# Hybrid encoder layer on one core: the first norm's operation on GpSimd, products of zeros in a pause, and the gating's norm scale and bias moved behind the mixing

## The chip, the cores and the metric

The kernel runs on 1 core of one Trainium2 chip. The time is the device time of one execution in microseconds (us). The core's engines have queues of their own: TensorE (PE, with its weight loads PEld), VectorE (DVE), ScalarE (ACT), GpSimd (POOL) and SyncE (SP), which here only issues DMAs. An engine works through its queue in order; semaphores tie the queues together.

## The reference, cut to what matters

One layer, one sequence of 512 tokens with 2048 channels, all in float32:

```
mod = silu(c) @ w_ada + b_ada;  shift, scale, gate = split(mod, 3)
h = layernorm(x) * (1 + scale) + shift
u, v, z_a, q, k, v_b, z_b = split(h @ w_in)            # 7168 columns
vg = layernorm(gelu(v), per channel group of 128) * norm_g + norm_b
sv = einsum('gpq,bnqgc->bnpgc', w_s, vg) + b_s          # mixes the 128 tokens of a chunk
y_a = gelu(u) * sv * silu(z_a)
y_b = neighbourhood_attention(q, k, v_b, rpb) * silu(z_b)
out = layernorm(alpha * x + (1 + gate) * (concat(y_a, y_b) @ w_out)) * ln_g + ln_b
```

For a channel c of group g the mixing is linear, so that the sum over q of w_s[p,q] * (n[q,c] * norm_g[c] + norm_b[c]) equals norm_g[c] * (the sum over q of w_s[p,q] * n[q,c]) + norm_b[c] * (the sum over q of w_s[p,q]).

## The kernel before, in words

Every float32 product is made of three products in a rounded float type: an operand is split into a high part (`h_hi`, `whi`) and a low part (`h_lo`, `wlo`), and high by high, high by low and low by high are summed in PSUM (`mm3`, L225; `mm_vz`, L238). ACT makes the high part of a weight block (L195), DVE or POOL the low part (L197).

**Start.** The four token tiles of x (128 tokens each) are loaded. For a tile n, `statistics` (L431, L432, DVE) gives mean and variance, `inverse` (L435, L436, POOL) the inverse deviation, and `normalise` (L444) the normalised tile in four quarters of 512 columns: all four on POOL for tiles 0 and 1, two on POOL and two on DVE for tiles 2 and 3. Each quarter is transposed by four TensorE products with the identity (L448) and copied back by ACT (L449), which gives channels by tokens.

**Modulation.** `w_ada` is read in tiles `wada` (ring of ADA = 6, L324). The 128 channels of k tile 0 get their scale and shift on TensorE (`ada_tensor`, L350, 64 hardware products); those of the other 15 k tiles on DVE (`ada_vector`, L367, L369, L375), closed by a product with ones (`ada_end`, L383) and an add (L384). `make_h` then makes `h_hi` and `h_lo` of the k tile (ACT L396 or L399/L400, DVE L397 and L401). `ada_before` says how many weight blocks of the plan are loaded before each `wada` tile; `pump` issues both kinds on SP in that order.

**First phase.** Projections start as soon as k tiles 0 and 1 exist (`first_segment`): all products that need k tile 0, then `advance(6)`, which closes the modulation of k tile 1, then those that need k tile 1. PSUM: `psm` is the ring of four banks that hold `res` (the open sums of VZ0), `psx` the ring of partial sums.

**Gating.** `sgu` runs twice, for two halves of 4 channel groups: DVE statistics per group (L552, L553), variance plus epsilon (L121, DVE), its inverse root (L122, POOL), the normalisation (L557, DVE), times `gB` and plus `bB` (L559, L560, POOL), then per group the mixing product (L566), plus the bias (L567, DVE), times y (L570, DVE). The first half runs beside the last segment of the first phase, where `psx` sums of z_a are taken up by DVE (L760, L765) and a bank of that ring becomes the fifth bank of `psm`; the second runs beside the last projection.

The queues' order is written by a scheduler from the program's order, except for instructions in `pin(...)`, which keep it. After the first phase come attention, the output projection and the last norm.

## Time and profile before

| | |
|---|---|
| time, median of 3 runs | 949.42 us (949.05 to 949.64) |
| the profiled execution's own time | 947.96 us |
| its span (first to last instruction) | 946.2 us |
| PE busy | 891.0 us (94%) |
| PEld, DVE busy | 773.6 us (82%), 603.9 us (64%) |
| POOL, ACT busy | 354.1 us (37%), 321.6 us (34%) |
| DMA | 145.6 MB, mean 154 GB/s |

Times in the profile are microseconds from the span's start. A product's row starts when it enters the array; its neighbour may start before it has ended, so what products cost is read from the distance of their starts. A bracket at the end of a row says how long the engine was idle before it, and what ended the wait. [...]

### The profile page before, as it was taken

What the parts mean: (1) busy time and instruction counts of PE and PEld (TensorE: products, weight loads), DVE (VectorE), ACT (ScalarE), POOL (GpSimd) and SP (SyncE); (2) the same over time, 40 slices, a digit from 0 to 9 for tenths busy, and PEclk for the clock granted to TensorE, in tenths of its full rate; (3) what the DMA queues carried; (4) which work ended last, traced back from release to release, by engine and by line L of the source; (5) the groups of instructions that cost most, each with busy time, mean ns of one, the idle gap of its engine ahead of it and who ended that gap; (6) DMA issues with size and microseconds to landing.
All of it is one profiled execution on the core that took longest, in us unless ns stands there. A gap on an engine that the chain in (4) does not pass through costs nothing.

```text
span 946.2 us, 11802 instructions
## 1 busy us (share of the span) xinstructions
PE 891.0 (94%) x4468; PEld 773.6 (82%) x4468; DVE 603.9 (64%) x843; ACT 321.6 (34%) x397; POOL 354.1 (37%) x242
## 2 busy tenths in 40 slices
PE   2879999989998999999999999999999999999994
PEld 1768888788796898889888988899888888888883
DVE  3175898773456655575767867786867834252667
ACT  1226323313353143452527152624154421122300
POOL 6634546623558152605242543444246000000035
PEclk9989999999999899999999999999999999999997
DMA  9479988963432223344444555444433383323313
GB/s 303 124 222 306 298 266 264 311 201 112 157 89 76 76 84 96 101 146 127 153 150 132 168 156 147 154 123 144 134 98 104 112 313 131 112 83 103 105 51 127
DMA packets 107787, 145.60 MB, mean 154 GB/s; under 512 B 6993, under 2 KB 78801, under 8 KB 106961
## 3 DMA queue, kind: packets, MB, share of 16 engines
q1 hardware_dynamic: 103120, 134.25, 44.9%
q10 hardware_dynamic: 4610, 10.59, 3.2%
q8 instruction: 35, 0.57, 0.3%
q14 instruction: 22, 0.18, 0.1%
HBM read 140.62 MB, written 4.19 MB: 153 GB/s over the span
## 4 chain that ended last, share of the span: by engine, by line
PE 81%; POOL 7%; DVE 5%; issue 3%; DMA 2%; ACT 1%; POOLq 0%; SPq 0%; ACTq 0%; DVEq 0%
PE psm L225 52%; PE psx L225 14%; PE psm L238 8%; POOL xt L444 2%; PE ada L350 1%; POOL wlo L197 1%; POOL xr L878 1%; DVE ada L369 1%; DMA raw<-in_w_in_dram 1%; PE psx L687 1%; PE psx L639 1%; PE psx L566 1%; PE psx L638 1%; PE psx L685 1%; POOL xr L879 1%
## 5 line engine op out<-in xcount | busy, mean ns | idle before, releaser
L195 ACT CAST whi<-raw 128x1024 fp32r<-128x1024 f32 x133 | 139.0, 1049 | 355.6 <-PE psm L225 225.1
L197 DVE TENSOR_TENSOR wlo<-raw,whi 128x1024 fp32r<-128x1024 f32 x95 | 131.9, 1391 | 160.2 <-ACT whi L195 144.7
L225 PE MATMUL psm<-h_hi,whi 128*128 128x512 f32 x444 | 175.8, 396 | 0.4 <-DVE klo L592 0.4
L225 PE MATMUL psm<-h_lo,whi 128*128 128x512 f32 x444 | 174.4, 393 | 0.0
L225 PE MATMUL psm<-h_hi,wlo 128*128 128x512 f32 x444 | 174.3, 393 | 0.0
L197 POOL TENSOR_TENSOR wlo<-raw,whi 128x1024 fp32r<-128x1024 f32 x38 | 91.6, 2416 | 114.7 <-ACT whi L195 82.2
L225 PE MATMUL psm<-whi,h_hi 128*128 128x512 f32 (+1 forms) x296 | 114.7, 388 | 0.0
L225 PE MATMUL psm<-wlo,h_hi 128*128 128x512 f32 (+1 forms) x296 | 114.0, 385 | 0.0
L225 PE MATMUL psm<-whi,h_lo 128*128 128x512 f32 (+1 forms) x296 | 114.0, 385 | 0.0
L225 PEld LDWEIGHTS psm<-h_hi,wlo 128*128 128x128 f32 x444 | 84.0, 190 | 18.1
L225 PEld LDWEIGHTS psm<-h_hi,whi 128*128 128x128 f32 x444 | 84.3, 190 | 16.0 <-issue 0.6
L225 PEld LDWEIGHTS psm<-h_lo,whi 128*128 128x128 f32 x444 | 84.4, 190 | 15.2
L238 PE MATMUL psm<-whi,h_hi 128*128 128x256 f32 x248 | 72.3, 293 | 8.0 <-DVE s L760 4.9
L238 PE MATMUL psm<-whi,h_lo 128*128 128x256 f32 x248 | 71.9, 292 | 4.6 <-DVE h_lo L401 4.6
L122 POOL TENSOR_TENSOR rs<-vareps,mhalf 128x1 f32<-128x1 f32 x4 | 4.4, 1098 | 184.5 <-DVE vareps L121 184.5
L238 PE MATMUL psm<-wlo,h_hi 128*128 128x256 f32 x248 | 71.9, 290 | 0.2 <-DVE wlo L197 0.2
L369 DVE SCALAR_TENSOR_TENSOR ada<-wada,c_sb,ada 128x512 f32<-128x512 f32 (+1 forms) x104 | 69.1, 715 | 2.1 <-DMA wada<-in_w_ada_dram 1.8
L225 PEld LDWEIGHTS psm<-wlo,h_hi 128*128 128x128 f32 x296 | 63.5, 215 | 8.4
L225 PEld LDWEIGHTS psm<-whi,h_lo 128*128 128x128 f32 x296 | 63.4, 214 | 8.5
L225 PEld LDWEIGHTS psm<-whi,h_hi 128*128 128x128 f32 x296 | 63.4, 214 | 8.5
L225 PE MATMUL psx<-h_hi,whi 128*128 128x512 f32 x160 | 63.5, 397 | 2.3 <-DVE y_b L475 2.0
L225 PE MATMUL psx<-h_hi,wlo 128*128 128x512 f32 x160 | 62.5, 390 | 1.3 <-POOL wlo L197 1.3
(199 smaller groups left out, 1690.9 us busy)
## 6 DMA issues: line engine op xcount, KB each, us to landing
wada<-in_w_ada_dram SPq DMA_DIRECT2D x128, 256.0 KB, 5.2
raw<-in_w_in_dram SPq DMA_DIRECT2D x128, 256.0 KB, 3.2
raw<-in_w_in_dram SPq DMA_DIRECT2D x48, 512.0 KB, 4.3
rawg<-in_w_ada_dram SPq DMA_DIRECT2D x32, 512.0 KB, 4.4
raw<-in_w_out_dram SPq DMA_DIRECT2D x32, 512.0 KB, 3.7
xt<-in_x_dram SPq DMA_DIRECT2D x8, 512.0 KB, 8.5
xr<-in_x_dram ACTq DMA_DIRECT2D x4, 1024.0 KB, 7.4
tt<-in_rpb_dram ACTq DMA_DIRECT2D x16, 128.0 KB, 2.2
```

What stands on the lines that cost most here:

```text
L195: nc.scalar.copy(out=hi, in_=raw)
L197: eng.tensor_tensor(out=low, in0=raw, in1=hi.bitcast(F32), op=ALU.subtract)
L225: nc.tensor.matmul(ps, lhsT=a, rhs=b, start=first and j == 0, stop=last and j == 2)
L238: nc.tensor.matmul(ps[:, t * w:(t + 1) * w], lhsT=a, rhs=b[:, cs], start=first and t == 0 and j == 0, stop=last and t == 1 and j == 2)
L350: pin(nc.tensor.matmul(pc[s], lhsT=wt[:, j - j0, s, :], rhs=c_sb[:, j:j + 1], start=j == 0, stop=j == NK - 1))
L369: nc.vector.scalar_tensor_tensor(out=even if j == NK - 2 else acc, in0=wt[:, j - j0], scalar=cj, in1=acc, op0=ALU.mult, op1=ALU.add)
L444: eng.tensor_scalar(out=xn[:, cs], in0=xn[:, cs], scalar1=mv[:, n, 0:1], scalar2=rstd[:, n:n + 1], op0=ALU.subtract, op1=ALU.mult)
L566: nc.tensor.matmul(ps[:, tok(n)], lhsT=v[n][:, tok(g)], rhs=wsT[:, g, :], start=True, stop=True)
L638: nc.tensor.matmul(po, lhsT=k2[:, h, keys], rhs=q2[:, h, q], start=True, stop=False)
L639: nc.tensor.matmul(po, lhsT=klo[:, h, keys], rhs=q2[:, h, q], start=False, stop=True)
L685: nc.tensor.matmul(ps[:, q], lhsT=v_hi[:, t, h, :], rhs=hi[:, sl], start=t == 0, stop=False, skip_group_check=True)
L687: nc.tensor.matmul(ps[:, q], lhsT=v_hi[:, t, h, :], rhs=lo[:, sl], start=False, stop=t == 3, skip_group_check=True)
```

## The change

1. **First norm.** DVE negates the mean and adds epsilon to the variance after each tile's statistics; POOL's inverse is one instruction in place of two; `normalise` adds the negative mean and multiplies (was: subtract and multiply), and keeps program order.
2. **Zeros.** A region of `h_lo` is set to zero at the start, and 14 products with these zeros as weights are added into `res[0]` ahead of `advance(6)` in `first_segment`. They change no value.
3. **Loads of `w_ada`.** The ring has 7 tiles, and for k tiles from 4 on a `wada` tile is due two weight blocks earlier.
4. **Gating.** The normalised v is mixed without `gB` and `bB` (8 POOL instructions less in each half). One more product per half, a 128x128 block of ones by the half's four spatial weights, gives their column sums; four DVE instructions (128x128) make norm_b times these sums plus b_s; the bias add behind each mixing product becomes multiply (norm_g) and add. norm_g and norm_b are loaded once as columns, 128 x 8 each.

```diff
-ADA = 6
+ADA = 7
+ZEROS = 14
...
-    one = const.tile([P, 1], F32, name="one")
-    nc.vector.memset(one, 1.0)
+    ones = const.tile([P, P], F32R, name="ones")
+    nc.vector.memset(ones.bitcast(F32), 1.0)
+    one = ones.bitcast(F32)[:, 0:1]
+    gb = const.tile([P, 2, 8], F32, name="gb")
+    nc.scalar.dma_start(out=gb[:, 0, :], in_=sgu_g)
+    nc.scalar.dma_start(out=gb[:, 1, :], in_=sgu_b)
...
-            ada_before += [2 if k0 == 1 else 5 * k0 // 2] * (4 * nk)
+            ada_before += [2 if k0 == 1 else 5 * k0 // 2 - 2 * (k0 > 2)] * (4 * nk)
...
+        zeros = h_lo[:, NK - 1, :P]
+        nc.vector.memset(zeros.bitcast(F32), 0.0)
...
             nc.vector.bn_aggr(out=mv[:, n, :], in_=st)
+            nc.vector.tensor_scalar(out=mv[:, n, 0:1], in0=mv[:, n, 0:1], scalar1=-1.0, scalar2=None, op0=ALU.mult)
+            nc.vector.tensor_scalar(out=mv[:, n, 1:2], in0=mv[:, n, 1:2], scalar1=EPS, scalar2=None, op0=ALU.add)
 
         def inverse(n):
-            nc.gpsimd.tensor_scalar(out=rstd[:, n:n + 1], in0=mv[:, n, 1:2], scalar1=1.0, scalar2=EPS, op0=ALU.mult, op1=ALU.add)
-            nc.gpsimd.tensor_tensor(out=rstd[:, n:n + 1], in0=rstd[:, n:n + 1], in1=mhalf[:, 0:1], op=ALU.pow)
+            nc.gpsimd.tensor_tensor(out=rstd[:, n:n + 1], in0=mv[:, n, 1:2], in1=mhalf[:, 0:1], op=ALU.pow)
...
-                eng.tensor_scalar(out=xn[:, cs], in0=xn[:, cs], scalar1=mv[:, n, 0:1], scalar2=rstd[:, n:n + 1],
-                                  op0=ALU.subtract, op1=ALU.mult)
+                pin(eng.tensor_scalar(out=xn[:, cs], in0=xn[:, cs], scalar1=mv[:, n, 0:1], scalar2=rstd[:, n:n + 1],
+                                      op0=ALU.add, op1=ALU.mult))
...
                 mm3(two[i], wv, i, 0, False, True, False)
+
+            for _ in range(ZEROS):
+                nc.tensor.matmul(res[0], lhsT=zeros, rhs=h_hi[:, 0, :], start=False, stop=False)
             advance(6)
...
-            nc.gpsimd.tensor_tensor(out=v[n], in0=v[n], in1=gB, op=ALU.mult)
-            nc.gpsimd.tensor_tensor(out=v[n], in0=v[n], in1=bB, op=ALU.add)
-            yield
+            yield
+        ps = bank()
+        nc.tensor.matmul(ps, lhsT=ones.bitcast(F32), rhs=flat, start=True, stop=True)
+        for g in range(4):
+            nc.vector.scalar_tensor_tensor(out=bs[:, g, :], in0=ps[:, tok(g)], scalar=gb[:, 1, half * 4 + g:half * 4 + g + 1], in1=bs[:, g, :],
+                                           op0=ALU.mult, op1=ALU.add)
         yield
...
-            nc.vector.tensor_tensor(out=sv, in0=ps.rearrange("p (n q) -> p n q", n=4),
-                                    in1=bs[:, g:g + 1, :].to_broadcast([P, 4, P]), op=ALU.add)
+            nc.vector.scalar_tensor_tensor(out=sv, in0=ps.rearrange("p (n q) -> p n q", n=4), scalar=gb[:, 0, half * 4 + g:half * 4 + g + 1],
+                                           in1=bs[:, g:g + 1, :].to_broadcast([P, 4, P]), op0=ALU.mult, op1=ALU.add)
```

What the change moves is seen in the queues' orders. Line numbers are those of the kernel in question (L435, L436, L444 before are L445, L453 after; L225 is L231, L238 is L244, L383 is L391, L122 is L128, L197 is L203). First TensorE in the pause of the first k tiles, before:

```order
L225 MATMUL psx<-whi,h_hi 128x512
L225 MATMUL psx<-wlo,h_hi 128x512
L225 MATMUL psx<-whi,h_lo 128x512
L383 MATMUL ada_111<-one,gate_89 128x1 x2
L238 MATMUL psm<-whi,h_hi 128x256
L238 MATMUL psm<-wlo,h_hi 128x256
```

And after:

```order
L231 MATMUL psx<-wlo,h_hi 128x512
L231 MATMUL psx<-whi,h_lo 128x512
L507 MATMUL psm<-h_hi,h_lo 128x512 x14
L391 MATMUL ada_115<-ones,gate_92 128x1 x2
L244 MATMUL psm<-whi,h_hi 128x256
L244 MATMUL psm<-wlo,h_hi 128x256
```

The 14 products of zeros stand ahead of the product that closes the modulation of k tile 1 (the one that reads `gate`, a scratch area). Next POOL's queue at the first gating, before (`rss` is the inverse root, `s` is v):

```order
L122 TENSOR_TENSOR rss<-vareps,mhalf 128x4
L559 TENSOR_TENSOR s<-s,gate_89 128x512
L122 TENSOR_TENSOR rss<-vareps,mhalf 128x4
L560 TENSOR_TENSOR s<-s,gate_89 128x512
L559 TENSOR_TENSOR s<-s,gate_89 128x512
L197 TENSOR_TENSOR wlo<-raw,whi 128x1024
L560 TENSOR_TENSOR s<-s,gate_89 128x512
L122 TENSOR_TENSOR rss<-vareps,mhalf 128x4
L559 TENSOR_TENSOR s<-s,gate_89 128x512
L560 TENSOR_TENSOR s<-s,gate_89 128x512
```

And after:

```order
L128 TENSOR_TENSOR rss<-vareps,mhalf 128x4
L203 TENSOR_TENSOR wlo<-raw,whi 128x1024
L128 TENSOR_TENSOR rss<-vareps,mhalf 128x4 x2
L203 TENSOR_TENSOR wlo<-raw,whi 128x1024
L128 TENSOR_TENSOR rss<-vareps,mhalf 128x4
L788 MEMSET gate_92 128x2048
```

The last inverse root still stands behind a weight split, but behind no scale or bias product. Last, TensorE where the last segment's sums end and the next projection begins, with buffer numbers (before: psx_2289 is the last bank of the last segment, psm_2414 the bank whose first product waits for DVE):

```order
L225 MATMUL psx_2289<-h_hi_87,wlo_2223 128x512
L238 MATMUL psm_2415<-whi_2293,h_hi_87 128x256
L238 MATMUL psm_2415<-wlo_2294,h_hi_87 128x256
L238 MATMUL psm_2415<-whi_2293,h_lo_88 128x256
L238 MATMUL psm_2415<-whi_2293,h_hi_87 128x256
L238 MATMUL psm_2415<-wlo_2294,h_hi_87 128x256
L238 MATMUL psm_2415<-whi_2293,h_lo_88 128x256
L238 MATMUL psm_2415<-whi_2293,h_hi_87 128x256
L238 MATMUL psm_2415<-wlo_2294,h_hi_87 128x256
L238 MATMUL psm_2414<-whi_2293,h_hi_87 128x256
```

After (psx_2416 is the bank of the column sums; psm_2433 gets 12 products and psm_2434 five before the first into psm_2432, which waits for DVE):

```order
L231 MATMUL psx_2305<-h_hi_90,wlo_2241 128x512
L573 MATMUL psx_2416<-gate1_92,ones_75 128x512
L244 MATMUL psm_2433<-whi_2309,h_hi_90 128x256
L244 MATMUL psm_2433<-wlo_2310,h_hi_90 128x256
L244 MATMUL psm_2433<-whi_2309,h_lo_91 128x256
L244 MATMUL psm_2433<-whi_2309,h_hi_90 128x256
```

The product with ones stands ahead of the next projection's, and 17 products instead of 8 stand ahead of the one that waits for DVE's take-up of the last segment.

## Rows read from the trace of the kernel before

**Rows 1.** Busy time of each engine by stretches of the span (us, then busy us and number of instructions of PE, PEld, DVE, ACT, POOL, then PEclk, the DMA engines' share, GB/s).

```profile
0.00:34.00 34.00, 12.28 (x46) 8.31 (x47) 11.80 (x25) 7.71 (x13) 24.27 (x23) 1.00 0.81 250
...
75.00:200.00 125.00, 118.84 (x587) 102.38 (x587) 99.26 (x148) 47.84 (x67) 63.24 (x32) 1.00 0.91 289
...
295.00:316.00 21.00, 14.63 (x64) 12.12 (x63) 12.45 (x19) 4.37 (x6) 11.15 (x6) 0.84 0.33 101
316.00:905.00 589.00, 588.57 (x3043) 512.41 (x3043) 376.23 (x471) 207.51 (x243) 171.90 (x133) 1.00 0.41 129
```

**Rows 2.** What TensorE waited for in the whole span (in total, times, longest).

```profile
PE psm L448 <- POOL xt L444: 21.2, 9, 12.6
PE psm L238 <- DVE s L760: 4.9, 1, 4.9
PE psm L238 <- DVE h_lo L401: 4.6, 2, 3.6
```

**Rows 3.** The chain of waits in the start (start, us, what): POOL's normalisation, then TensorE without a gap.

```profile
10.46 8.25 POOL xt L444 x4
...
18.80 0.19 POOL rstd L435
...
19.74 8.24 POOL xt L444 x4
...
29.00 4.65 POOL xt L444 x2
...
33.70 1.11 PE psm L448 x4
34.81 3.63 PE ada L350 x18
...
44.84 6.63 PE ada L350 x32
```

**Rows 4.** Groups of instructions on POOL by shape (busy us, mean ns of one | idle before).

```profile
L444 POOL TENSOR_SCALAR xt<-xt,mv,rstd 128x512 f32<-128x512 f32 x12 | 25.5, 2138 | 0.4
L645 POOL COPY x<-s 128x128 f32<-128x128 f32 x16 | 15.9, 993 | 69.9 <-DVE s L640 66.5 <-DMA raw<-in_w_in_dram 3.4
L473 POOL TENSOR_TENSOR s<-gate,s 128x512 f32<-128x512 f32 x12 | 15.3, 1294 | 1.5 <-ACT gate L472 1.5
```

**Rows 5.** The DMA engines and the others from 14 to 38 us, columns as in rows 1.

```profile
14.00:28.00 14.00, 6.69 (x24) 4.29 (x24) 1.79 (x4) 3.90 (x7) 13.71 (x9) 1.00 1.13 307
28.00:38.00 10.00, 8.47 (x37) 7.30 (x37) 3.74 (x7) 2.93 (x5) 9.47 (x8) 1.00 0.01 3
```

**Rows 6.** TensorE in the pause of the first k tiles, in order of time (start, us, engine, line, operation, count, idle before).

```profile
54.57 0.63 PE L225 MATMUL psm<-h_lo,whi 128*128 128x512 f32 x1
55.00 0.63 PE L225 MATMUL psm<-h_hi,whi 128*128 128x512 f32 x1
...
60.23 0.40 PE L225 MATMUL psx<-whi,h_lo 128*128 128x512 f32 x1
61.78 0.61 PE L383 MATMUL ada<-one,gate 128*128 128x1 f32 x4 [1.15 <-DVE gate L375]
63.49 0.58 PE L238 MATMUL psm<-whi,h_hi 128*128 128x256 f32 x1 [1.10 <-ACT h_hi L396]
...
67.42 0.58 PE L238 MATMUL psm<-whi,h_lo 128*128 128x256 f32 x1 [1.00 <-DVE h_lo L401]
...
72.71 0.52 PE L225 MATMUL psx<-whi,h_hi 128*128 128x512 f32 x1
```

**Rows 7.** TensorE's granted clock in and behind that pause, columns as in rows 1.

```profile
62.00:63.00 1.00, 0.39 (x4) 0.30 (x3) 0.58 (x2) 0.38 (x1) 0.00 (x0) 0.87 1.01 337
67.00:72.00 5.00, 4.58 (x15) 4.00 (x16) 5.00 (x9) 1.14 (x2) 0.02 (x1) 0.50 0.55 155
73.00:76.00 3.00, 3.00 (x14) 2.89 (x14) 2.97 (x6) 1.28 (x3) 1.38 (x1) 1.00 1.05 351
```

**Rows 8.** POOL and DVE at the end of the first gating, in order of time.

```profile
295.84 2.38 POOL L197 TENSOR_TENSOR wlo<-raw,whi 128x1024 fp32r<-128x1024 f32 x1
298.17 1.29 POOL L560 TENSOR_TENSOR s<-s,gate 128x512 f32<-128x512 f32 x1
299.42 1.02 POOL L122 TENSOR_TENSOR rss<-vareps,mhalf 128x4 f32<-128x4 f32 x1
...
300.48 1.11 DVE L557 TENSOR_SCALAR s<-s,mvs,rss 128x128 f32<-128x128 f32 x4 [4.57 <-POOL rss L122]
```

**Rows 9.** TensorE at the same place.

```profile
298.27 0.50 PE L225 MATMUL psx<-h_hi,wlo 128*128 128x512 f32 x1 [1.27 <-POOL wlo L197]
...
303.92 0.39 PE L238 MATMUL psm<-wlo,h_hi 128*128 128x256 f32 x1 [0.24 <-DVE wlo L197]
309.87 0.58 PE L238 MATMUL psm<-whi,h_hi 128*128 128x256 f32 x1 [4.85 <-DVE s L760]
...
315.70 1.05 PE L566 MATMUL psx<-gate,s 128*128 128x128 f32 x8
```

**Rows 10.** The chain of waits behind that place (four mixing products of 128 columns, 8 in the hardware).

```profile
315.86 0.89 PE psx L566 x8
```

**Rows 11.** DVE where the last k tiles are made, in order of time.

```profile
189.49 0.75 DVE L367 TENSOR_SCALAR ada<-wada,c_sb 128x512 f32<-128x512 f32 x1 [2.75 <-DMA wada<-in_w_ada_dram]
191.53 3.11 DVE L401 TENSOR_TENSOR h_lo<-xt,h_hi 128x512 fp32r<-128x512 f32 x2
```

More of the change, by code (lines that the diff above doesn't have):

```diff
@@ L536, in hybrid_kernel, with sgu @@
     rings["x"][0] = ps_x.enter_context(tc.tile_pool(name="ps_x1", bufs=4, space=PSUM))
-    def sgu(half, v, y, gB, bB, wsT, bs, sv):
+    def sgu(half, v, y, wsT, bs, sv):
         hs = slice(half * 512, (half + 1) * 512)
+        flat = wsT
         wsT, bs, sv = [t.rearrange("p (g q) -> p g q", g=4) for t in (wsT, bs, sv)]
-        nc.scalar.dma_start(out=gB, in_=sgu_g[:, hs].to_broadcast([P, 512]))
-        nc.scalar.dma_start(out=bB, in_=sgu_b[:, hs].to_broadcast([P, 512]))
         nc.scalar.dma_start(out=wsT, in_=w_sp[:, half * 4:(half + 1) * 4, :])
@@ L770, in gating @@
     def gating():
-        yield from sgu(0, acc_v, y_a0, *scratch, y_b[0][3])
+        yield from sgu(0, acc_v, y_a0, *scratch[:2], y_b[0][3])
         nc.gpsimd.memset(gate1, 0.0)
@@ L794, in gate_sum @@
     def gate_sum(pool):
-        ones = pool.tile([P, P], F32R, name="ones")
-        nc.vector.memset(ones.bitcast(F32), 1.0)
         for i in range(4):
@@ L827, in hybrid_kernel @@
     with tc.tile_pool(name="sg1", bufs=1) as sg:
-        gtiles = [sg.tile([P, 512], F32, name=f"sgp{i}") for i in range(5)]
+        gtiles = [sg.tile([P, 512], F32, name=f"sgp{i}") for i in range(3)]
         def gate_and_sgu():
@@ L968, in _layout @@
         "w_in": a["w_in"].reshape(2048, 7168),
-        "sgu_g": a["sgu_norm_g"].reshape(1, 1024),
-        "sgu_b": a["sgu_norm_b"].reshape(1, 1024),
+        "sgu_g": a["sgu_norm_g"].reshape(8, 128).T,
+        "sgu_b": a["sgu_norm_b"].reshape(8, 128).T,
         "w_sp": w_sp.reshape(128, 8, 128),
```

## The prediction

> **What bounds the kernel.** I read the busy table by stretches first. From 316 to 905 us TensorE is busy 588.57 of 589 us: there nothing but TensorE's own work counts, and whatever is won or lost earlier is carried whole to the end [rows 1]. It is not the bound before 34 us (12.28 of 34) and not from 295 to 316 (14.63 of 21, clock 0.84); from 75 to 200 it lacks 6.2 of 125 us while the DMA engines are at 0.91 [rows 1]. The list of its waits names the three places: POOL's normalisation (21.2 us), DVE's take-up of the last segment (4.9), DVE's `h_lo` (4.6) [rows 2]. The change touches each. So every edit is priced by how much earlier or later TensorE runs on behind it.
>
> **Part 1, the first norm.** The chain goes through POOL without a gap: four quarters in 8.25 us, the inverse, four in 8.24, the inverse, two in 4.65 up to 33.65; from 33.70 TensorE works off transposes and the 64 products of k tile 0 without idling [rows 3]. The ten POOL quarters cost 21.1 us, 2.1 each; these are on the path, and nothing hides them. The last two quarters (tile 3) are covered by the first half of the k tile's products.
>
> What an add costs there no row shows. This is one input of 512 elements at 2.1 us, while POOL's add of *two* inputs of the same size takes 1.29 [rows 4]: the subtract-and-multiply form is slow in itself, slower than an instruction that reads twice as much. I take 1.29 for add-and-multiply, its nearest row by operation and size: 10 x (2.11 - 1.29) = 8.2 us. The bounds are 2.1 (the same work under another name, nothing gained) and, on the fast side, TensorE: four transposes take 1.11 us [rows 3], so the 48 ahead of k tile 0 need 12 x 1.11 = 13.3 us, against 12 quarters in 23.2 now, which caps the gain near 10. Slower than 2.1 cannot be excluded: the dearest POOL row by element, a strided copy of 128 elements in 0.993 us [rows 4], would be 4.0 us for 512.
>
> POOL also loses one instruction per tile: three of them on the chain, each 0.19 plus a gap of 0.08 (18.80 to 19.07), 0.8 us [rows 3]. For the first tile DVE's two additions of one column stand where POOL's instruction stood, and I count them alike; pinning lets tile 3's statistics go before DVE's quarters, which ends no wait on the chain. Sum of part 1: **-9.0** (0 to -10).
>
> The gain needs `w_ada`'s first tiles sooner, at about 26 instead of 35 us. The DMA engines are full until 28 us and idle from 28 to 38 (0.01) [rows 5]; k tile 0's eight loads stand in SP's queue ahead of three weight blocks and four more loads, which end there too, so they have landed. From then on the loads wait for buffers that TensorE frees, and move with it.
>
> [...]
>
> **Part 2, the zeros.** Before, TensorE ends k tile 0's products at 60.5 (60.23 plus one distance of 0.23), waits 1.15 us for DVE and closes k tile 1's modulation at 61.78; it waits 1.10 for `h_hi` and 1.00 for `h_lo`, and runs on from 67.42 [rows 6]. The granted clock falls in between and is 0.50 until about 72.7; from 73 it is 1.00 [rows 7]. (At 55 us products of 512 columns are 0.43 apart, at 60 us 0.23, though the column says 1.00; there I trust the distances [rows 6].) The 14 products at 0.23 take 3.2 us, so the closing product, queued behind them, starts at 63.7 instead of 61.78. It delays `modc`, `h_hi` and `h_lo` by 1.9: 67.42 becomes 69.3. What follows up to 72.71 is 5.3 us at half clock, of which two products (0.86) now come earlier. If the clock stays up, the remaining 4.4 become 2.2 and the same point comes at 71.5, 1.2 earlier; if it falls all the same (TensorE still stands more than a microsecond for each of `h_hi` and `h_lo`) it comes at 73.7, 1.0 later. I take **0**. The upper bound is zeros at half clock, 14 x 0.43 = 6.0 us, the closing product 4.7 late.
>
> **Part 3, loads of `w_ada`.** The longest `h_lo` wait, 3.6 us [rows 2], ends at 194: DVE's queue stands 2.75 us for a `wada` tile before it comes to `h_lo` [rows 11]. A seventh buffer and an earlier turn take aim at that. At 0.91 of the DMA engines [rows 1] an earlier tile makes a weight block later: 512 KB at 289 GB/s is 1.8 us. I take **-1.5** (-3.6 to +1.8).
>
> **Part 4, the first gating.** POOL's last inverse root runs at 299.42, behind a split (295.84) and a bias add (298.17); DVE has stood 4.57 us for it at 300.48, and queued behind on DVE are two weight splits and the take-up of the last segment, for which TensorE stands 4.85 [rows 8, 9]. With two smaller waits TensorE idles 1.27 + 0.24 + 4.85 = 6.36 us there. Then its 16 products of 256 columns and 6 of 512 take 309.87 to 315.70, 5.83 us; at full clock (0.23 apart for 512 columns [rows 6], half of that for 256) they take 3.3, so 2.5 more go to the clock [rows 9].
>
> Without scale and bias the inverse roots follow their variances, and the split ends at about 295.9, the last root at 296.9, 3.5 us sooner; DVE's operations also no longer run beside those of POOL. What is late next is that root behind the split. It would leave some 1.3 us of the 4.85, but now 17 products, not 8, stand before the one that waits: 9 more, about 1.6 us of cover. The new product with ones waits only for the first bank's take-up, which comes in time if DVE is 3 us earlier. It costs TensorE four times 128 columns, as the four mixing products: 0.89 [rows 10]. Sum -6.36 - 2.5 + 0.9 = -8.0; I keep half a microsecond of waiting, **-7.5** (-8 to -5, the last if the clock falls anyway).
>
> **Part 4, the second gating.** It lies in the stretch where TensorE never idles, so POOL's eight instructions and DVE's four cost or give nothing, and the product with ones is paid in full: **+0.9**.
>
> **Sum.** -9.0 + 0 - 1.5 - 7.5 + 0.9 = -17.1 us. The profiled execution took 947.96 and would take 930.9; the median, 1.46 above it, goes from 949.42 to **932.3**.
>
> **Rivals.**
> - *The add costs what the subtract costs.* For it: both forms read one input and do two operations. Against it: the 1.29 us row of a two-input add. Part 1 falls to -0.8, the sum to -8.9: 940.5 us.
> - *The first gating's wait is replaced.* TensorE stands at the product with ones until DVE has taken up the first bank, and the clock falls as before. For it: that product stands ahead of all the next projection's work, where before 8 products could still run. Against: DVE's 4.57 us of standing still goes. Part 4 gives -1 instead of -7.5: 938.8 us.
> - *Slower than before: add-and-multiply is a dearer path on POOL.* Place: the same ten quarters. For it: the strided copy's 7.8 ns per element, 4.0 us per quarter; against it the 2.5 ns of the add. With the other parts at -8.9 it decides from 2.11 + 0.89 = 3.0 us per quarter on; at 4.0 the chain is 18.9 us longer and the time 959.4.
>
> **How the numbers follow.** Forecast 0.58, add as dear as subtract 0.25, replaced wait 0.08, dearer add 0.04; the rest, 0.05, is parts 2 and 3 both at their dear ends on top of a dear add (-8.9 + 4.7 + 3.3 = -0.9, no change). The forecast's own range adds the ends of parts 1 and 4 and those of 2 and 3: 928 to 937. With the two next cases and a margin below 940.5 and above, 928 to 943 holds the time 8 times in 10. A measurement of this kernel tells 0.2% (1.9 us) from no change. The first three cases are all faster by more than that, 0.91; slower is 0.04, no change 0.05.
>
> **What would show it.** Part 1: POOL's quarters near 1.3 us, TensorE's first `w_ada` product near 26 us; quarters at 2.1 mean the first rival. Part 2: products of zeros 0.23 apart, and the clock column at 1.00 or 0.50 behind them. Part 3: the wait for `h_lo` before the last k tiles. Part 4: no DVE wait over 2 us for the inverse root, no clock drop behind the last segment, and 0.9 us for each product with ones. The forecast is wrong if TensorE gets new waits between 75 and 300 us that eat what the start gives, which would say that the DMA engines bound that stretch.

## The result and the profile after

The changed kernel took **920.0 us** (median of 4 runs, 915.96 to 920.80) against 949.23 before; the ratio is 0.9688, its 95% interval 0.9656 to 0.972. Forecast were 932.3 us and a range from 928 to 943: the direction was right, the gain nearly twice the forecast one. The profiled execution took 919.98 us, its span is 918.2.

POOL in the start of the changed kernel, in order of time (start, us, engine, line, operation, count):

```profile
10.42 3.01 POOL L453 TENSOR_SCALAR xt<-xt,mv,rstd 128x512 f32<-128x512 f32 x4
...
14.05 3.01 POOL L453 TENSOR_SCALAR xt<-xt,mv,rstd 128x512 f32<-128x512 f32 x4
...
17.68 1.78 POOL L453 TENSOR_SCALAR xt<-xt,mv,rstd 128x512 f32<-128x512 f32 x2
```

Four quarters take 3.01 us where they took 8.25 [rows 3]: **0.75 us each** (2.1 before, 1.29 forecast). A tile now costs POOL 3.63 us (10.42 to 14.05). DVE needs nearly as long for the next tile's statistics, 2.93, and TensorE for a tile's 16 transposes 3.44 at half clock (PEclk, the granted share of TensorE's full clock, 0.50 there; 0.21 each), so a still faster POOL would win little. One quarter is late for another reason. DVE makes the first quarter of tile 2 behind the statistics of tile 3:

```profile
18.37 1.38 DVE L453 TENSOR_SCALAR xt<-xt,mv,rstd 128x512 f32<-128x512 f32 x2
```

The inverse root that it needs was there at 17.58 (17.03 plus 0.55).

TensorE from there to the first segment, in order of time:

```profile
19.01 1.94 PE L457 MATMUL psm<-ident,xt 128*128 128x128 f32 x16 [1.16 <-ACT xt L458]
20.78 4.06 PE L358 MATMUL ada<-c_sb,wada 128*128 128x1 f32 x32
24.71 3.65 PE L457 MATMUL psm<-ident,xt 128*128 128x128 f32 x16
28.15 6.83 PE L358 MATMUL ada<-c_sb,wada 128*128 128x1 f32 x32
...
43.12 3.36 PE L507 MATMUL psm<-h_hi,h_lo 128*128 128x512 f32 x14
46.33 0.50 PE L391 MATMUL ada<-ones,gate 128*128 128x1 f32 x4
...
51.85 0.38 PE L244 MATMUL psm<-whi,h_lo 128*128 128x256 f32 x1 [1.78 <-DVE h_lo L409]
...
55.42 0.63 PE L231 MATMUL psx<-whi,h_hi 128*128 128x512 f32 x1 [0.96 <-ACT s L478]
...
58.47 0.40 PE L231 MATMUL psx<-h_hi,whi 128*128 128x512 f32 x1
```

The first modulation product starts at 20.78 instead of 34.61 (34.81 as the chain of [rows 3] puts it). Sixteen transposes take 1.77 us from 19.01 on but 3.44 from 24.71 on; the 32 products of one column 3.93 and then 6.83. That is the clock: PEclk is 1.00 from 19 to 23 us and 0.50 from 24 to 40 us, so the first of each ran at full clock, but for the end of the 32 products, the second at half. The products of zeros (L507) are 0.23 apart and end 1.1 us after DVE's gate, which the closing product (L391) needs:

```profile
44.83 0.42 DVE L383 TENSOR_TENSOR gate<-ada,gate 128x256 f32<-128x256 f32 x1
```

The wait of 1.16 us ahead of the transposes from 19.01 on is put down to an ACT copy, but ACT's copies had ended at 18.56. What ended just before 19.01 is DVE's quarter, at 18.91, so it is the likely cause.

The stretches of the changed kernel, columns as in [rows 1], first one inside the second:

```profile
25.00:28.00 3.00, 3.00 (x16) 3.00 (x15) 0.00 (x0) 1.63 (x3) 0.00 (x0) 0.50 1.19 299
20.80:43.10 22.30, 20.21 (x106) 19.48 (x105) 8.03 (x18) 6.92 (x10) 6.45 (x4) 0.62 1.04 305
43.10:58.50 15.40, 11.56 (x56) 10.02 (x55) 14.47 (x24) 4.36 (x6) 4.78 (x3) 1.00 0.98 317
58.50:231.00 172.50, 169.11 (x813) 145.69 (x812) 119.35 (x179) 60.47 (x81) 85.90 (x48) 1.00 0.74 236
...
280.00:290.00 10.00, 9.47 (x60) 8.00 (x59) 7.76 (x13) 3.57 (x5) 0.00 (x0) 1.00 0.39 123
290.00:877.00 587.00, 586.57 (x3025) 510.09 (x3024) 367.41 (x472) 206.63 (x243) 157.69 (x125) 1.00 0.40 129
```

From 43 to 877 us the granted clock stays at 1.00 now; the drops of [rows 7] (to 0.50) and at the first gating (0.84 in [rows 1]) are gone. What TensorE still waits for (in total, times, longest):

```profile
PE psm L457 <- POOL xt L453: 11.2, 1, 11.2
PE psm L244 <- ACT whi L201: 2.1, 1, 2.1
...
PE psm L244 <- DVE h_lo L409: 1.8, 1, 1.8
```

Of the three places of [rows 2] the first is one wait of 11.2 us, for the first quarter of all; the 3.6 us for `h_lo` before the last k tiles and the 4.85 us in the first gating are gone. There, TensorE's rows now read (answering to [rows 9]):

```profile
280.87 1.02 PE L573 MATMUL psx<-gate,ones 128*128 128x512 f32 x2
281.33 0.69 PE L244 MATMUL psm<-whi,h_hi 128*128 128x256 f32 x1
281.85 0.28 PE L244 MATMUL psm<-wlo,h_hi 128*128 128x256 f32 x1
...
285.01 0.35 PE L244 MATMUL psm<-whi,h_hi 128*128 128x256 f32 x1 [0.53 <-DVE gate L575]
```

The product with ones costs 0.46 us and makes the next product 0.40 longer than usual (0.52 to 0.12): 0.86. The only wait left is half a microsecond for the new DVE multiply. DVE's longest wait for an inverse root there, 4.57 us before [rows 8], is now 1.19:

```profile
274.11 1.12 DVE L569 TENSOR_SCALAR s<-s,mvs,rss 128x128 f32<-128x128 f32 x4 [1.19 <-POOL rss L128]
```

**Where the time went**, by four stretches that end at TensorE's marks: **S1** to the first product of k tile 0's modulation, **S2** to the end of k tile 0's products (the first product of zeros; where there are none, the last product plus one distance), **S3** to the first segment's first `h_hi,whi` product in `psx`, **S4** to the end of the span. All are differences of row starts in each kernel's profile; medians are over 4 runs each (before: 3).

| kernel | S1 | S2 | S3 | S4 | span | median |
|---|---|---|---|---|---|---|
| before | 34.6 | 25.9 | 15.2 | 870.6 | 946.2 | 949.4 |
| changed | 20.8 | 22.3 | 15.4 | 859.7 | 918.2 | 920.0 |
| changed, again (a2) | 20.7 | 19.1 | 15.4 | 860.4 | 915.6 | 918.6 |
| e1, subtract | 33.3 | 22.3 | 15.4 | 858.8 | 929.8 | 933.0 |
| e2, before with the add | 21.6 | 20.7 | 16.1 | 871.6 | 929.9 | 931.8 |
| e3, no zeros | 20.8 | 17.4 | 15.5 | 859.2 | 913.0 | 916.5 |
| e7, 9 zeros | 20.8 | 22.4 | 14.6 | 859.8 | 917.6 | 917.6 |
| e4, old loads | 21.1 | 19.1 | 15.4 | 864.7 | 920.2 | 924.6 |
| e8, six buffers | 20.7 | 17.4 | 15.4 | 864.9 | 918.3 | 920.3 |
| e8, old due | 20.7 | 19.1 | 15.4 | 859.3 | 914.5 | 916.2 |
| e5, old gating | 20.7 | 22.4 | 15.3 | 866.5 | 924.9 | 926.1 |
| e9, more zeros in S2 | 20.5 | 24.9 | 16.6 | 859.6 | 921.6 | 920.3 |
| e10, early products, 9 zeros | 21.7 | 20.7 | 14.7 | 859.9 | 917.0 | 919.1 |

The span fell by 28.0 us: 13.8 in S1, 3.5 in S2, -0.2 in S3, 10.8 in S4. Between kernels that are alike in a stretch S1 and S3 agree within some 0.6 us (e9 and e10 apart) and S4 within 1.6, so each edit is read from its own stretch. S2 does not agree.

S4 is split once more, at the product that closes the last modulation, first before, then after:

```profile
230.73 0.95 PE L383 MATMUL psx<-one,gate 128*128 128x1 f32 x8
```

```profile
209.41 0.95 PE L391 MATMUL psx<-ones,gate 128*128 128x1 f32 x8
```

Up to it S4 took 155.1 us (from 75.65) and takes 150.9 (from 58.47): 4.1 us of the gain lie where the loads act, 6.7 behind, where the gatings lie.

### The profile page after: what moved, and what is told of

Read it like the earlier page. It is cut to its first block, busy times and chain, and to the rows that moved or that the text cites. A ratio compares the mean times of both kernels' runs of the same rounds, so it can differ in the third digit from the quotient of the medians.

```text
span 918.2 us, 11832 instructions
## 1 busy us (share of the span) xinstructions
PE 881.2 (96%) x4486; PEld 767.8 (84%) x4486; DVE 595.4 (65%) x859; ACT 321.1 (35%) x397; POOL 310.4 (34%) x222
## 4 chain that ended last, share of the span: by engine, by line
PE 64%; POOL 2%; issue 1%; DVE 1%; ACT 1%; DMA 0%; POOLq 0%; SPq 0%; DVEq 0%; ACTq 0%
PE psm L231 52%; PE psm L244 7%; POOL xr L891 1%; PE psx L702 1%; PE psx L654 1%; PE psx L653 1%; PE psx L581 1%; PE psx L700 1%; POOL xr L892 1%; PE psx L701 1%; POOL rs L128 0%; DMA raw<-in_w_in_dram 0%; ACT xr L890 0%; DVE wlo L203 0%; POOLq L1007 0%
## 5 line engine op out<-in xcount | busy, mean ns | idle before, releaser
L203 DVE TENSOR_TENSOR wlo<-raw,whi 128x1024 fp32r<-128x1024 f32 x95 | 130.4, 1375 | 161.9 <-ACT whi L201 148.5
L231 PE MATMUL psm<-h_hi,whi 128*128 128x512 f32 x444 | 175.4, 395 | 0.4 <-DVE klo L607 0.4
L231 PE MATMUL psm<-h_lo,whi 128*128 128x512 f32 x444 | 173.7, 391 | 0.0
L231 PE MATMUL psm<-h_hi,wlo 128*128 128x512 f32 x444 | 173.2, 390 | 0.0
L203 POOL TENSOR_TENSOR wlo<-raw,whi 128x1024 fp32r<-128x1024 f32 x38 | 91.7, 2420 | 107.8 <-ACT whi L201 82.0
L231 PE MATMUL psm<-whi,h_hi 128*128 128x512 f32 (+1 forms) x296 | 114.7, 388 | 0.0
L231 PE MATMUL psm<-wlo,h_hi 128*128 128x512 f32 (+1 forms) x296 | 114.0, 385 | 0.0
L231 PE MATMUL psm<-whi,h_lo 128*128 128x512 f32 (+1 forms) x296 | 114.0, 385 | 0.0
L231 PEld LDWEIGHTS psm<-h_hi,wlo 128*128 128x128 f32 x444 | 83.3, 188 | 17.9
L231 PEld LDWEIGHTS psm<-h_hi,whi 128*128 128x128 f32 x444 | 83.8, 189 | 16.2 <-issue 0.8
L231 PEld LDWEIGHTS psm<-h_lo,whi 128*128 128x128 f32 x444 | 83.9, 189 | 15.3 <-issue 0.2
L244 PE MATMUL psm<-whi,h_hi 128*128 128x256 f32 x248 | 71.2, 288 | 3.7 <-ACT whi L201 2.1
L128 POOL TENSOR_TENSOR rs<-vareps,mhalf 128x1 f32<-128x1 f32 x4 | 4.4, 1096 | 203.2 <-DVE vareps L127 203.2
L244 PE MATMUL psm<-whi,h_lo 128*128 128x256 f32 x248 | 70.1, 284 | 1.8 <-DVE h_lo L409 1.8
L231 PEld LDWEIGHTS psm<-wlo,h_hi 128*128 128x128 f32 x296 | 63.5, 215 | 8.5
L231 PEld LDWEIGHTS psm<-whi,h_hi 128*128 128x128 f32 x296 | 63.4, 214 | 8.6
L231 PEld LDWEIGHTS psm<-whi,h_lo 128*128 128x128 f32 x296 | 63.4, 214 | 8.3
L244 PE MATMUL psm<-wlo,h_hi 128*128 128x256 f32 x248 | 70.1, 283 | 0.0
L231 PE MATMUL psx<-h_hi,whi 128*128 128x512 f32 x160 | 63.5, 397 | 2.5 <-DVE y_b L484 2.0
L231 PE MATMUL psx<-h_lo,whi 128*128 128x512 f32 x160 | 62.4, 390 | 0.0
```

The costliest lines, as they stand in the source:

```text
L203: eng.tensor_tensor(out=low, in0=raw, in1=hi.bitcast(F32), op=ALU.subtract)
L231: nc.tensor.matmul(ps, lhsT=a, rhs=b, start=first and j == 0, stop=last and j == 2)
L244: nc.tensor.matmul(ps[:, t * w:(t + 1) * w], lhsT=a, rhs=b[:, cs], start=first and t == 0 and j == 0, stop=last and t == 1 and j == 2)
```

## The experiments

**The operation (e1).** The changed kernel with the positive mean subtracted:

```diff
-            nc.vector.tensor_scalar(out=mv[:, n, 0:1], in0=mv[:, n, 0:1], scalar1=-1.0, scalar2=None, op0=ALU.mult)
-                                       op0=ALU.add, op1=ALU.mult))
+                                       op0=ALU.subtract, op1=ALU.mult))
```

> The changed kernel with the positive mean subtracted in the first norm, as before; DVE's negation of the mean goes with it. TensorE's order is that of the changed kernel. Theory A (the operation alone makes the price: add-and-multiply 0.75 us per quarter, subtract-and-multiply 2.1): POOL's quarters are at 2.07 to 2.14 us again, the 48th transpose ends 13 to 14 us later (near 34.5 us instead of 20.78), TensorE is at half clock in k tile 0's first products, and the time is about 920 + 14 + 2.5 = 936.5 us. Theory B (the quarters became short because of the new order of DVE's statistics and POOL's work at the start, not because of the operation): quarters stay at 0.75 us and the time stays within 2 us of 920.

The POOL quarters of e1, and those of the changed kernel (count: shortest/median/longest in ns, first and last start):

```profile
L452 POOL TENSOR_SCALAR xt<-xt,mv,rstd x12: 2071/2077/2346, 10.2 to 35.3; 128x512 f32<-128x512 f32 x12
```

```profile
L453 POOL TENSOR_SCALAR xt<-xt,mv,rstd x12: 767/767/1036, 10.4 to 21.3; 128x512 f32<-128x512 f32 x12
```

Theory A holds: the time is 933.0 us, S1 is 12.5 us longer, and the other stretches are within a microsecond of the changed kernel's. S1 is 1.3 us shorter than before the change, which is what the rest of the change to the first norm brings (forecast 0.8). S2 stayed as in the changed kernel, so the 2.5 us that theory A added for the clock did not come.

**The add alone (e2).** The kernel before, and nothing else changed than:

```diff
+            nc.vector.tensor_scalar(out=mv[:, n, 0:1], in0=mv[:, n, 0:1], scalar1=-1.0, scalar2=None, op0=ALU.mult)
-                                  op0=ALU.subtract, op1=ALU.mult)
+                                  op0=ALU.add, op1=ALU.mult)
```

> The kernel before with one part alone: DVE negates the mean, and the first norm adds it and multiplies. Zeros, loads of w_ada, gating and the epsilon on POOL are as before. Theory A (operation alone): POOL's quarters take 0.75 us, ten of them on the chain save 13.5 us, TensorE's dense transposes bring the clock up in the first k tile for another 2 us or so: about 949.2 - 16 = 933 us, and the waits before the last k tiles (3.6 us for h_lo) and in the first gating (4.85 us) stay as they were. Theory B (order, not operation): quarters stay near 2.1 us, 949 us. Theory C (what the start gives is lost between 75 and 231 us, because the loads fill that stretch): quarters 0.75 us, but the last first-stage product comes less than 10 us earlier than before, about 940 us.

The time is 931.8 us, the ratio 0.9819 (0.9789 to 0.9849): theory A. S1 fell by 13.0 and S2 by 5.2; S3 rose by 0.9 and S4 by 1.0. So little of the start is taken back where the DMA engines are busy (against theory C), and the add alone brings more than half of the whole gain. The microsecond in S4 is lost at one place: TensorE waits 3.58 us for the `h_lo` of the last k tiles, as before, but behind it the clock falls, where the kernel before had 1.00 ([rows 1], 75 to 200 us):

```profile
176.00:180.00 4.00, 3.33 (x16) 3.33 (x17) 4.00 (x7) 0.00 (x0) 0.07 (x1) 0.57 0.84 259
```

**Which forms are cheap (e6).** One run, with instructions on scratch tiles, each form twice. They ran beside the second gating, where TensorE hides them (it is busy for all 40 us from 682 to 722), not ahead of the first:

```diff
+        for o0, o1 in ((ALU.subtract, ALU.mult), (ALU.add, ALU.mult), (ALU.mult, ALU.add), (ALU.mult, ALU.subtract)):
+            for _ in range(2):
+                pin(nc.gpsimd.tensor_scalar(out=fout, in0=fsrc, scalar1=col, scalar2=col, op0=o0, op1=o1))
+        for o0 in (ALU.subtract, ALU.add, ALU.mult):
+            for _ in range(2):
+                pin(nc.gpsimd.tensor_scalar(out=fout, in0=fsrc, scalar1=col, scalar2=None, op0=o0))
+                ...
+                pin(nc.gpsimd.tensor_tensor(out=fout, in0=fsrc, in1=fsrc2, op=o0))
```

> The changed kernel with instructions added to GpSimd ahead of the first gating, on tiles of 128x512 of their own whose values nothing uses, each form twice: with one column per operand subtract-multiply, add-multiply, multiply-add, multiply-subtract; with one column alone subtract, add, multiply; with two whole inputs subtract, add, multiply. So GpSimd is late there and the time as a whole says nothing. Theory A (a subtract with a column operand is dear, wherever it stands): 2.07 us for subtract-multiply, multiply-subtract and the single subtract; 0.75 us for all with add and multiply; 1.3 us for the three of two inputs, subtract among them. Theory B (only add-multiply and the like of a multiply and an add are made fast, everything else is slow, the single operations too): single add and single multiply at 2 us as well. Theory C (the price of the kernel before was that of its place, beside DVE's work and loads): subtract-multiply 0.75 us here.

POOL in e6, single instructions in order of time: subtract-multiply twice, the second add-multiply, the second multiply-add, the second multiply-subtract, then the second single subtract, and the second multiply of two inputs.

```profile
682.11 2.09 POOL L848 TENSOR_SCALAR form<-form,mhalf 128x512 f32<-128x512 f32 x1
684.30 3.62 POOL L848 TENSOR_SCALAR form<-form,mhalf 128x512 f32<-128x512 f32 x1
...
690.15 0.77 POOL L848 TENSOR_SCALAR form<-form,mhalf 128x512 f32<-128x512 f32 x1
...
691.90 1.09 POOL L848 TENSOR_SCALAR form<-form,mhalf 128x512 f32<-128x512 f32 x1
...
696.64 2.08 POOL L848 TENSOR_SCALAR form<-form,mhalf 128x512 f32<-128x512 f32 x1
...
701.15 1.56 POOL L851 TENSOR_SCALAR form<-form,mhalf 128x512 f32<-128x512 f32 x1
...
719.87 1.63 POOL L854 TENSOR_TENSOR form<-form,form 128x512 f32<-128x512 f32 x1
```

Theory B comes nearest, with one correction. The pairs of multiply and add are the fast ones, in either order (0.77 and 0.78 at best); a pair with a subtract costs 2.08 to 2.09 at best wherever the subtract stands (against C: also here). But the single subtract costs no more than the single add or multiply (1.56 to 1.57 at best, not 2), so the subtract is not dear by itself (against A): **one operation alone takes twice as long as multiply and add together** (1.56 to 0.77). Two inputs took 1.63 to 1.65 at best for all three operations (the add of [rows 4] 1.29, in another place). The longer one of two equal instructions (3.62 to 2.09) ran while DVE was busy without a break (3.70 of 3.70 us); that DVE caused it was not tested, and the first multiply-subtract took 3.45 with DVE busy for about half of that time (1.66 of 3.60 us). What in GpSimd makes the pairs differ no run shows.

**Zeros (e3, e7).**

```diff
-ZEROS = 14
+ZEROS = 0    (e3; 9 in e7)
```

> The changed kernel without the 14 products of zeros between k tile 0 and k tile 1's modulation. Theory A (the zeros hold the clock): the closing product runs some 1.1 us earlier, but the granted clock falls to 0.50 before the first h_lo product and what follows costs 2 to 3 us more; the time is 1 to 2 us longer, 921 to 922 us. Theory B (they only delay the closing product, because with the shorter start the clock would stay up anyway): the clock stays at 1.00 and the time is about 1 us shorter, 919 us.

> The changed kernel with 9 products of zeros in place of 14 between k tile 0 and the closing product of k tile 1's modulation. Theory A (14 are some 5 too many: they end 1.1 us after DVE's gate is there, 9 end with it): from the end of k tile 0's products to the first h_hi,whi product of the first segment 14.3 us in place of 15.35, with the clock at 1.00 throughout; time some 1 us shorter than with 14. Theory B (9 do not hold the clock): it falls to 0.50 as without zeros, the stretch is 15.5 us as there, and the time is that of the kernel without zeros.

Without zeros TensorE reads, in order of time:

```profile
20.84 3.63 PE L358 MATMUL ada<-c_sb,wada 128*128 128x1 f32 x32
...
26.11 3.63 PE L358 MATMUL ada<-c_sb,wada 128*128 128x1 f32 x32
...
40.06 0.61 PE L391 MATMUL ada<-ones,gate 128*128 128x1 f32 x4 [1.64 <-DVE gate L383]
```

and the clock behind the pause:

```profile
43.00:51.00 8.00, 6.19 (x19) 4.40 (x19) 8.00 (x11) 1.86 (x3) 2.84 (x2) 0.57 1.10 352
```

The clock falls, as theory A says, but it costs nothing in sum: S3 is 15.5 against 15.4 us, because the closing product comes earlier by what the clock takes back. With 9 zeros S3 is 14.6 (and 14.7 in e10), so 0.7 us of the 1.05 that theory A gave come, though the clock falls here too for a while, which theory A had excluded:

```profile
46.50:50.50 4.00, 3.25 (x10) 2.43 (x10) 4.00 (x5) 1.63 (x2) 2.29 (x1) 0.63 1.01 323
```

The median of e3, 916.5 us, lies below both of its theories' times and 3.5 us below the changed kernel's. Its profile doesn't put that down to the zeros: it gains 4.9 us in S2, ahead of the place where the zeros stood.

**S2 (a2).** Whether that is chance, the changed kernel itself had to tell:

> The changed kernel itself, beside the others on the same chip. The kernels with its first norm so far differ in the first 40 us: from the 48th transpose to the end of k tile 0's products they took 22.3 us (changed kernel), 17.4 (without zeros) and 19.1 (old loads), according to when the granted clock fell and rose in that stretch, though the work there is the same. Theory A (that point differs from execution to execution): this second profile shows another length of that stretch, between 17 and 23 us, and the runs are spread over some 5 us around 918. Theory B (it belongs to the kernel, as the zeros or the buffers place it): 22.3 us again, and 920 us.

```profile
20.74 3.70 PE L358 MATMUL ada<-c_sb,wada 128*128 128x1 f32 x32
...
27.67 3.80 PE L358 MATMUL ada<-c_sb,wada 128*128 128x1 f32 x32
...
39.80 3.36 PE L507 MATMUL psm<-h_hi,h_lo 128*128 128x512 f32 x14
```

Theory A holds. The second 32 products took 3.80 us where the first profile of the same kernel has 6.83; S2 is 19.1 instead of 22.3. In all kernels whose start is the same S2 is 17.4, 19.1 or about 22.4 us, and the spans differ by that. So the time of one execution carries up to 5 us of where the clock falls and rises before 43 us, and medians of four runs that differ by less than some 3 us say nothing on an edit by themselves.

**Keeping the clock up (e9, e10).** e9 adds products of zeros whose result is not used among those of one column; e10 puts 20 of them at the very start. The product of e9 (e10's is alike):

```diff
+                pin(nc.tensor.matmul(fill[0], lhsT=zeros, rhs=h_lo[:, NK - 1, :], start=True, stop=True))
```

> The changed kernel with more products of zeros, 512 columns each, whose result is not used: two after each of the four tiles of w_ada in k tile 0's modulation and eight more at its end, where TensorE waits for h_hi and weights anyway. In the changed kernel's profile the clock falls to 0.50 at 24 us, while TensorE does k tile 0's modulation (products of one column, which are issued without a gap) and transposes, and is back at 1.00 at 41 us. Theory A (with wide products between them the clock stays at 1.00): from the 48th transpose to the end of k tile 0's products 17 us or less in place of 22.3, every execution, and 915 us. Theory B (the clock falls all the same): the added products cost 8 x 0.23 to 0.43 us ahead of the modulation, 2 to 4 us, and the time is 920 to 923.

> The changed kernel with 9 products of zeros in k tile 1's pause in place of 14, and 20 products of zeros of 512 columns, whose result is not used, at the very start, where TensorE waits 11 us for the first normalised quarter. Theory A (TensorE's clock in the first 45 us follows what TensorE did shortly before): the transposes from 11 us on run at 0.12 us in place of 0.21, and the stretch of half clock that lay from 24 to 41 us in the changed kernel moves or shrinks; the first segment's first h_hi,whi product comes at 55 us or sooner in place of 57.8. Theory B (the half clock from 24 us on comes whatever TensorE did before): the stretch lies where it lay, and the time is 917 to 918.5, that of 9 zeros alone. Theory C (early work brings the fall forward): TensorE is at half clock already from 15 to 20 us and the time is longer than 918.5.

By windows, columns as in [rows 1], first e9, then e10:

```profile
24.00:40.00 16.00, 16.00 (x66) 14.93 (x66) 2.88 (x7) 5.75 (x8) 0.63 (x1) 0.50 0.96 270
```

```profile
11.00:25.00 14.00, 11.35 (x79) 9.67 (x79) 10.82 (x25) 6.75 (x12) 11.68 (x16) 0.88 1.05 318
25.00:40.00 15.00, 12.91 (x61) 12.24 (x62) 4.65 (x11) 5.89 (x8) 2.43 (x1) 0.54 0.99 298
```

For e9 theory B holds: TensorE was busy for all 16 us and the clock was low all the same; S2 is 2.5 us longer, S3 1.2. e10 fits none of its theories well. The long stretch of half clock comes about where it came (0.54 from 25 to 40 us; 0.62 from 20.8 to 43.1 in the changed kernel), which is nearest to theory B, but the clock falls once more ahead of it (0.88 from 11 to 25 us). S2 is 20.7, and S1 is 0.9 longer because x was there 0.9 us later (DVE's statistics begin at 7.40 instead of 6.49). The time, 919.1 us, is above the 917 to 918.5 of theory B. As S2 differs between executions of one kernel, one profile can't tell whether the early products moved anything in it. What sets the clock in S2 stays open.

**Loads (e4, e8).** Both edits of the loads undone, then each alone:

```diff
-ADA = 7
+ADA = 6
-            ada_before += [2 if k0 == 1 else 5 * k0 // 2 - 2 * (k0 > 2)] * (4 * nk)
+            ada_before += [2 if k0 == 1 else 5 * k0 // 2] * (4 * nk)
```

> The changed kernel with w_ada's loads as before: six buffers, and the due rule of before. Theory A (the seventh buffer and the earlier turn removed the waits between 75 and 231 us): the h_lo wait of about 3.6 us before the last k tiles is there again, and the time is some 4 us longer, 924 us. Theory B (the earlier start alone moved the loads out of the way of each other): no such wait, and the time is within 1 us of 920.

> The changed kernel with six buffers for w_ada in place of seven and the new due rule. TensorE's order is the same. With both edits of the loads undone, the stretch from the first segment's first h_hi,whi product to the end took 864.7 us, against 859.7 with both. Theory A (the earlier turn acts): no h_lo wait of 3.7 us, 860 us in that stretch. Theory B (the seventh buffer acts, because without it an earlier turn finds no free tile): the wait is there, 864 to 865 us. Theory C (each does half): about 862 us.

> The changed kernel with seven buffers and the due rule of before. Theory A (the earlier turn acts): the h_lo wait of some 3.7 us is there, 864 to 865 us from the first segment's first h_hi,whi product to the end. Theory B (the seventh buffer acts): no such wait, 860 us. Theory C (each does half): about 862 us.

TensorE's wait for `h_lo` with six buffers, and with seven and the old due rule (in total, times, longest):

```profile
PE psm L244 <- DVE h_lo L409: 5.5, 2, 3.7
```

```profile
PE psm L244 <- DVE h_lo L409: 1.8, 1, 1.8
```

S4 is 864.7 without both, 864.9 with six buffers, 859.3 with seven and the old rule: the **seventh buffer** is worth 5 us and the due rule nothing. Of the 5 us 3.7 are the wait; the rest fits the clock, which falls behind it as in e2. With six buffers:

```profile
169.00:176.00 7.00, 5.79 (x25) 5.60 (x26) 6.46 (x9) 0.00 (x0) 0.61 (x1) 0.51 0.96 300
```

The wait begins on DVE; with six buffers, in order of time:

```profile
164.10 0.75 DVE L375 TENSOR_SCALAR ada<-wada,c_sb 128x512 f32<-128x512 f32 x1 [1.25 <-DMA wada<-in_w_ada_dram]
...
167.09 0.76 DVE L377 SCALAR_TENSOR_TENSOR ada<-wada,c_sb,ada 128x512 f32<-128x512 f32 x1 [1.65 <-DMA wada<-in_w_ada_dram]
167.76 3.00 DVE L409 TENSOR_TENSOR h_lo<-xt,h_hi 128x512 fp32r<-128x512 f32 x2
```

DVE stands for two `wada` tiles just ahead of `h_lo`, as in [rows 11]. With seven buffers it waits longer for such tiles in sum (7.2 us from 58 to 235 us in the changed kernel, 4.8 here), but not ahead of an `h_lo` that TensorE stands for.

**Gating (e5).** The changed kernel with the gating of before:

```diff
+            nc.gpsimd.tensor_tensor(out=v[n], in0=v[n], in1=gB, op=ALU.mult)
+            nc.gpsimd.tensor_tensor(out=v[n], in0=v[n], in1=bB, op=ALU.add)
-        nc.tensor.matmul(ps, lhsT=ones.bitcast(F32), rhs=flat, start=True, stop=True)
...
```

> The changed kernel with the gating as before: norm scale and bias on POOL, row layout of the parameters, no product with ones. Norm, zeros and loads stay as changed. Theory A (the first gating gave what was forecast): from the end of the last segment's products to the first mixing product TensorE stands some 5 us for DVE again, the granted clock falls there, and the stretch from the first whi,h_hi... psx product of the first segment to the end is 6 to 7 us longer than in the changed kernel (859.7 us in its profile); the second gating gives 0.9 back within that. Time 926 to 927 us. Theory B (with DVE no longer waiting for w_ada ahead of it, the gating had no long wait any more, and the shorter stretch between 231 and 300 us comes from the loads): no wait over 2 us there, time within 2 us of 920.

```profile
289.46 0.58 PE L241 MATMUL psm<-whi,h_hi 128*128 128x256 f32 x1 [4.86 <-DVE s L769]
```

```profile
DVE s L566 <- POOL rss L125: 4.6, 1, 4.6
```

The time is 926.1 us, S4 6.8 us longer: theory A. The wait of 4.86 us, those of 1.2 for POOL's split and ACT's gate, and the clock (0.89 from 270 to 300 us) are back as in the kernel before, so what the loads do earlier has no part in it.

## Why the prediction was off

The change acted at the places that were forecast; the sum was 11 us short (28.0 in the profiled span, 17.1 forecast). Part 1 lacks 4.8 of them, S2, which had no term, 3.5, and part 3 2.6.

- **Part 1** (forecast -9.0) is the step that failed. "I take 1.29 for add-and-multiply, its nearest row by operation and size" priced a quarter at 1.29 us; it takes 0.75, and 10 x (2.11 - 0.75) + 0.8 = 14.4 is near what S1 shows (-13.8). The 0.6 between them fit DVE's late quarter of tile 2: the prediction says that the pinned order "ends no wait on the chain", but by the trace it makes one (not tested). The row was near by name only: it was another form, with two inputs. The range could not reach there, because the second bound was mis-read as well: "four transposes take 1.11 us [rows 3], so the 48 ahead of k tile 0 need 12 x 1.11" took the length of four lone transposes for their rate; dense they take 0.11 us each at full clock (1.77 for 16) and about 0.21 at half (3.44). At half clock the 48 need 10.1 us, so the cap lay near 13, not near 10, and the changed kernel comes up to it: its 48 transposes take 9.5 us (11.24 to 20.78), 1.16 of them the wait.
- That the first rival ("add costs what the subtract costs") had 0.25 was the same error from the other side. That "both forms read one input and do two operations" spoke for it, and yet the add-multiply row shows 767 ns and the subtract-multiply row 2077 (e1); what makes them differ was not shown.
- **S2** had no term. I moved k tile 0's products as they were, 25.9 us, at half clock by the distances of those of 512 columns (0.43 at 55 us [rows 6]). They take 17.4 to 22.4 now; e2 shows a gain with the add alone (20.7). Before, TensorE stood for POOL between most groups of four transposes ([rows 2]: nine waits, 21.2 us); now the transposes of a tile follow each other without a gap, and the sixteen from 19.01 us on already run at full clock (1.77 us, PEclk 1.00). In the profile shown the gain is 3.5 us; how much of it one execution gets differs from the next.
- **Part 2** (0) is right in size, but in part by luck: the clock stayed up (1.00 from 43.1 to 58.5 us), and for that case the prediction's working gives -1.2. A longer wait for `h_lo` (1.78 us for 1.00) and a new one for an ACT copy (0.96) stand against that. Against none, 14 zeros bring 0.2 us in S3 as a whole; the closing product comes 3.2 us after k tile 0's products, without zeros 1.8 (e3): 1.4 late, not 1.9, because DVE's gate is later, too.
- **Part 3** (-1.5) had the right wait and the wrong size: 4.1 us in the profiles, 5 where the loads are undone in the changed kernel, both more than its far end of -3.6. I let a late weight block take back half; none was late. It is one edit of the two that acts.
- **Part 4** (-7.5 and +0.9) is right: -6.7 for both in the profiles and -6.8 by e5, forecast -6.6; the product with ones costs 0.86.

Parts 3 and 4, each undone in the changed kernel, give 5.0 + 6.8 = 11.8, the profile 10.8. The 1.0 between them fits the clock behind the wait for `h_lo`: it fell with six buffers (0.51) and in e2 (0.57), but not in the kernel before (1.00). Why it stayed up there is not shown.

The experiments point to 9 zeros (e7, 917.6 us). It beats the kernel before by 3% (ratio 0.9693, 0.9654 to 0.9733), and in S3 the changed kernel by 0.7 us; in whole runs that is within what S2 scatters, so no version is shown to be faster than the changed one.

## What to carry to other kernels

Price an instruction by a row of the very form (one input or two, one operation or two, and which pair); where no row has it, a range that reaches from a fraction of the nearest row to a multiple of it is honest, and a cap is only a cap if it is a rate. On GpSimd, at 128x512 float32 with column operands, turning a subtract beside a multiply into an add of a negated column took an instruction from 2.08 to 0.77 us here; a lone add or multiply took 1.57, so it may gain by becoming a pair (not tried in place). Compare edits by stretches between marks of the bounding engine: a single number for the whole run hid an effect of 5 us here behind another of the same size (e8 with six buffers: 920.3 us, with S2 4.9 shorter and S4 5.2 longer than in the changed kernel).

## What was not expected of the hardware

- GpSimd, 128x512 float32, column operands: multiply and add together 0.77 us (0.75 from start to start), either alone 1.57, a pair with subtract 2.08 (e1, e6).
- TensorE's granted clock fell at 24 us (from 1.00 to 0.50) although TensorE had been busy without a gap from 19 us on, in executions of one kernel for different lengths (S2 22.3 and 19.1 us), with wide products among the narrow ones too (e9: 0.50 from 24 to 40 us).
- Behind the same wait of 3.6 to 3.7 us for `h_lo` the clock stayed at 1.00 in the kernel before and fell to about half in e2 (0.57) and with six buffers (0.51).
- With nine products of zeros the pause was 0.7 us shorter than with fourteen (S3 14.6 and 15.4 us), although the clock fell for part of it (0.63 from 46.5 to 50.5 us).
